# A smaller delay factor for the background scan steps of a first-layer mixer

## Chip, cores, metric

The kernel runs on one core of one Trainium2 chip. The metric is the device time of one execution in microseconds (us). Three runs of the kernel before gave 3419.37, 3421.62 and 3433.52 us, so its median is 3421.62 us.

## What is computed

Two blocks follow each other over 512 tokens of width 1024 (`x`) with 256 context tokens beside them in the first. The change touches only the first layer of the first block, whose mixer is a spatial gate beside a bidirectional linear recurrence (8 heads of 64, two directions, context first, then `x`). Cut to that:

```python
def rwkv7_scan(r, w, k, v, kk, b, s0):
    def step(s, inp):
        r_t, w_t, k_t, v_t, kk_t, b_t = inp
        sa = jnp.einsum('bhvk,bhk->bhv', s, kk_t)
        s = s * w_t[:, :, None, :] - sa[..., None] * b_t[:, :, None, :] + v_t[..., None] * k_t[:, :, None, :]
        return s, jnp.einsum('bhvk,bhk->bhv', s, r_t)
...
def mixer_ab(hc, hl, need_ctx, w_in, w_out, ...):
    pc, pl = hc @ w_in, hl @ w_in
    bc, bl = rwkv_bidir(pc, pl, ...)          # the scans, both directions, then norm, bonus and gate
    yl = jnp.concatenate([spatial_gate(pl, ...), bl], axis=-1) @ w_out
    yc = jnp.concatenate([spatial_gate(pc, ...), bc], axis=-1) @ w_out
```

## The kernel before

The recurrence is done in chunks of 64 tokens with a triangular inverse in each (`inverse`, L731 to L749). Two heads make a pair, and a pair with both its directions is a strand, `rwkv_pair`: a Python generator that emits one step (some 16 matmuls of 64x64 and their evictions) and then yields two numbers, the TensorE time of the step and the time until its results are there. There are four strands, one for each pair. Their products with the weights (`mmacc`, L344, L347 and L348: three matmuls for each K-tile) run in the foreground, in float32r pieces.

A planner inside the kernel mixes the two. It keeps a clock `now` of its own, in modelled ns; a step of the inverse, for one, yields 320 and 1000. After each K-tile of products `tick` adds the time of its matmuls, and every strand whose due time has come emits its next step there. After a step the due time is set by one line, where `s[3]` is the factor of that strand and LF is 2.5:

```python
s[2] = self.now + r[1] * LF * s[3]
```

Five parts follow each other on TensorE, and I call them by these names:

- **Projection part**: `proj(1)` to `proj(3)`, the products of the pairs 1 to 3; strands 0 and 1 begin beside them, with the factor SL1.
- **Gate part**: `gate_part`, the products of the spatial gate, beside the same strands and factor.
- **Early part**: no products. `finish(early)` runs strands 0 and 1 to their end (factor SLO, 1.2) together with strands 2 and 3 (factor 1.0) and with `ada_steps`, which reads the modulation weights in 40 steps of 1 MB (`ar`, L556 and L558). In this part the planner emits whatever is due first, one step behind the other.
- **Output part**: the product with `ab_w_out` over the first six of its eight K-tiles (`gemm_out`), beside what is left of strands 2 and 3 and of `ada_steps`.
- **Rest**: `drain` runs strands 2 and 3 to their end, and the last two K-tiles of the output product follow.

The order on TensorE is the planner's: the first matmul of each step and each K-tile is pinned in place, and the scheduler of the framework fills in the others. TensorE takes its queue in that order, so a step whose inputs are late holds up all that stands behind it. SP is the queue that issues nearly all DMAs, also in order: weights (`wr`), modulation weights (`ar`) and the strands' blocks (`kq`, `cut`). Slabs of the output weights and the modulation weights share two buffers `wr`; every third modulation step takes a pair `wh`, `wl` of the buffers for split weights instead.

Of the kernel before, what the change touches and what calls it, by code (L numbers as in the profile page):

```python
# [649 lines left out]

NB = 2
SLO = 1.2
SL1 = 0.9


class Chunk:
# [125 lines left out]
def mixer_ab(K, X, CH, x):  # L782
# [91 lines left out]
    def strand(pair, **pages):  # L874
        K.lend([envs[pair]], **pages)
        K.background(envs[pair], rwkv_pair(K, CH, pair, rkv, lo, Y), 8000, SL1 if pair < 2 else 1.0,
                     heirs[pair] if pair < 2 else None)
# [27 lines left out]
    for e in envs[:2]:  # L905
        K.give_back(e)

    K.env = Env((5, 6, 7), [], [], [])
    ks = range(KD - 2)
    y = gemm_out(K, K.ins["ab_w_out"][0], reload_split(K, Y, SEGS, ks), SEGS, ks)  # L910
# [11 lines left out]
def rwkv_pair(K, CH, p, rkv, lo, Y):  # L922

    nc = K.nc
    upt = K.p1(name="up")
    up = {}
    for i, key in enumerate(("b_w_up", "b_a_up")):
        up[key] = upt[:, i * P:(i + 1) * P]
        nc.gpsimd.dma_start(up[key], K.ins[key][0, :, :, p * P:(p + 1) * P].rearrange("d r c -> (d r) c"))
    y = {s: K.pg(s, name="y") for s, _ in SEGS}  # L930
    bon = {s: K.pg(s, name="bon") for s, _ in SEGS}
    pads = CH.pads(K.p1)

    SV, NV = [[K.p1(name=x) for _ in range(2)] for x in ("SV", "NV")]
    for h, t in enumerate(SV):
        nc.gpsimd.memset(t[64 * h:64 * h + 64], 0.0)
    seen = set()
    blk = C64 * NB
    ends = []

    def end(s, sel):
        ends.append(False)
        return rwkv_end(K, p, s, sel, y[s], bon[s], rkv, ends, len(ends) - 1)

    for s, n in reversed(SEGS):
        for i in range(0, n, blk):
            loc = ((s, i), (s, n - blk - i))
            out = {}
            yield from rwkv_prep(K, CH, p, loc, rkv, lo, up, bon, seen, out, pads, SV, NV)
            yield from rwkv_scan(K, loc, y, seen, out, SV, NV)  # L950
            if s == "c" and i == n - blk:
                K.background(K.env, end(s, slice(0, 2)))
            elif s == "l" and i == n - 2 * blk:
                K.background(K.env, end(s, slice(1, 3)))
    K.free(upt, *pads, *SV, *NV)
    yield from end("l", slice(0, 4, 3))
    while not all(ends):
        yield 0, 500
    for s, n in SEGS:
        K.free(bon[s])  # L960
        if p >= 2 and s == "l":
            Y[s][4 + p] = K.common_split(y[s])
        else:
            Y[s][4 + p] = K.out_dram(y[s], n)
# [1267 lines left out]
def program(K):  # L2232
# [8 lines left out]
    X = K.normed(x, SEGS, K.gs_pre(0, SEGS, "nmp0", 1), {s: K.modv(0, s, 0) for s, _ in SEGS})  # L2241
    K.vec_setup(layer1_vecs(K))
    y, xd = mixer_ab(K, X, CH, x)
    K.vec_setup(ffn_vecs(K, 0))

# [61 lines left out]
```

## Time and profile before

| | |
|---|---|
| runs | 3419.37, 3421.62, 3433.52 us (median 3421.62) |
| profiled execution | 3418.44 us, of which the profile's span is 3416.7 us |
| TensorE busy | 3151.7 us (92%) |
| VectorE, ScalarE, GpSimd busy | 2122.4 us (62%), 1269.4 us (37%), 614.0 us (18%) |
| mean granted TensorE clock | 0.953 |
| projection, gate, early, output part, rest, last two K-tiles | 123 to 250, to 394, to 700, to 801, to 848, to 866 us |

The parts were placed by the starts of their first and last products in the trace. The busy times of TensorE come from modelled ends of pipelined matmuls, so only its longer pauses show as idle. A matmul of the strands in float32 stands as two records in the trace, so a step that the order below prints as x8 is an x16 there.

### The profile page before, as it was taken

The numbers are of one execution on the slowest core, as the hardware profiler recorded it, in microseconds if no ns is written. First come the engines' busy times: TensorE is split into PE (matmuls) and PEld (weight loads), VectorE is DVE, ScalarE is ACT, GpSimd is POOL, SyncE is SP. The second block draws the span as 40 slices with busy tenths as digits, with TensorE's granted clock in tenths as the row PEclk, the third lists the DMA queues.
The fourth block names the chain that finished last, engine by engine and source line by source line (L and its number), as shares of the span: only waits on it lengthen the run. The fifth ranks groups of instructions, "written<-read, shape, count | busy, mean of one in ns | idle before, by whom it ended". The sixth has DMA issues, their size and how long they took to land.

```text
span 3416.7 us, 61935 instructions
## 1 busy us (share of the span) xinstructions
PE 3151.7 (92%) x25042; PEld 2476.2 (72%) x25042; DVE 2122.4 (62%) x4318; ACT 1269.4 (37%) x2679; POOL 614.0 (18%) x762
## 2 busy tenths in 40 slices
PE   7999898888899999989888999988999899999988
PEld 4878676667688888868765888767667567766756
DVE  4444565645855555685666576677777666677665
ACT  4333343333432222364433332352433335233332
POOL 4111222211000000010010000005156000525500
PEclk8999998999999999999998999989999899999979
DMA  6432554431222222122222223232232343123332
GB/s 228 141 94 70 166 167 155 139 112 52 73 72 68 72 73 97 57 73 69 81 78 82 91 87 132 78 99 78 69 103 95 104 138 102 57 69 108 102 115 90
DMA packets 313570, 336.10 MB, mean 98 GB/s; under 512 B 26542, under 2 KB 259132, under 8 KB 313284
## 3 DMA queue, kind: packets, MB, share of 16 engines
q1 hardware_dynamic: 311172, 329.69, 30.0%
q8 instruction: 197, 3.23, 0.4%
q0 software_dynamic: 2112, 2.45, 0.3%
q14 instruction: 89, 0.73, 0.1%
HBM read 282.13 MB, written 49.94 MB: 97 GB/s over the span
## 4 chain that ended last, share of the span: by engine, by line
PE 61%; issue 18%; DVE 14%; ACT 3%; DMA 3%; POOL 0%; SPq 0%; DVEq 0%; POOLq 0%; ACTq 0%
PE mm L344 14%; PE mm L347 13%; PE mm L348 13%; DVE cfa L1794 3%; PE ps L739 2%; PE ps L748 2%; PE ps L1192 2%; DVE wl L81 2%; PE ps L1137 1%; PE ps L558 1%; PE ps L1719 1%; PE ps L2133 1%; DMA ld<-sp 1%; PE ps L2160 1%; PE ps L1701 1%
## 5 line engine op out<-in xcount | busy, mean ns | idle before, releaser
L344 PE MATMUL mm<-hl,wh 128*128 128x512 f32 (+1 forms) x3296 | 1249.6, 383 | 56.0 <-DVE qkv L1794 15.2
L347 PE MATMUL mm<-hl,wh 128*128 128x512 f32 (+1 forms) x3296 | 1225.8, 372 | 1.6 <-DVE hl L487 1.6
L348 PE MATMUL mm<-hl,wl 128*128 128x512 f32 (+1 forms) x3296 | 1218.5, 372 | 0.0
L344 PEld LDWEIGHTS mm<-hl,wh 128*128 128x128 f32 x3296 | 631.1, 192 | 192.8 <-issue 33.2
L348 PEld LDWEIGHTS mm<-hl,wl 128*128 128x128 f32 x3296 | 631.4, 192 | 114.6 <-issue 2.8
L347 PEld LDWEIGHTS mm<-hl,wh 128*128 128x128 f32 x3296 | 633.2, 192 | 106.3 <-DVE hl L487 3.4
L80 ACT ACTIVATE wh<-wr 128x512 fp32r<-128x512 f32 (+3 forms) x718 | 367.9, 561 | 704.2 <-PE mm L347 614.3
L81 DVE TENSOR_TENSOR wl<-wr,wh 128x512 fp32r<-128x512 f32 (+3 forms) x718 | 435.7, 640 | 230.1 <-ACT wh L80 205.2
L1372 DVE SCALAR_TENSOR_TENSOR cv<-mm,vecs,cv 128x441 f32<-128x441 f32 (+2 forms) x352 | 242.9, 692 | 94.3 <-ACT cv L1360 88.2
L1423 POOL MEMSET gwh<- 128x1024 f32 x3 | 2.9, 955 | 969.2 <-PE mm L347 969.2
L1794 DVE SCALAR_TENSOR_TENSOR cfa<-ld,vecs,cfa 128x497 f32<-128x497 f32 (+14 forms) x160 | 162.1, 1013 | 13.2 <-ACT cfa L1788 11.0
L1962 POOL TENSOR_SCALAR tap<-ld,vecs 128x498 f32<-128x498 f32 (+4 forms) x80 | 150.6, 1882 | 63.9 <-PE ps L2046 29.8
L1395 DVE TENSOR_TENSOR fy<-fy,mm 128x512 f32<-128x512 f32 x96 | 55.2, 577 | 126.3 <-PE mm L348 125.5
L1963 POOL TENSOR_TENSOR cfa<-cfa,tap 128x498 f32<-128x498 f32 (+4 forms) x80 | 112.1, 1401 | 5.3
L743 ACT ACTIVATE pad<-ps 128x256 f32<-128x256 f32 (+1 forms) x100 | 46.7, 468 | 155.5 <-PE ps L739 155.0
L2138 ACT ACTIVATE u<-ps,beT 64x128 f32<-64x128 f32 x128 | 46.2, 362 | 131.3 <-DVE u L2137 130.6
L1374 ACT ACTIVATE cv<-cv,vecs 128x256 f32<-128x256 f32 (+1 forms) x66 | 43.0, 652 | 132.1 <-DVE cv L1372 77.2
L749 DVE TENSOR_TENSOR cut<-cut,ps 128x256 f32<-128x256 f32 x120 | 49.3, 413 | 54.0 <-PE ps L748 53.2
L2137 DVE TENSOR_SCALAR u<-ps,kdT 64x128 f32<-64x128 f32 x128 | 44.5, 349 | 58.4 <-PE ps L2133 44.4
L1378 DVE TENSOR_TENSOR cv<-cv,mm 128x512 f32<-128x512 f32 x66 | 39.5, 599 | 65.5 <-ACT cv L1374 36.2
L425 PE MATMUL ps<-sq,one 128*128 128x512 f32 (+1 forms) x132 | 62.6, 609 | 15.8 <-ACT sq L395 13.7
L731 POOL TENSOR_TENSOR pad<-L,zm 128x512 f32<-128x512 f32 x40 | 54.4, 1360 | 113.4 <-PE ps L739 84.0
(479 smaller groups left out, 4418.9 us busy)
## 6 DMA issues: line engine op xcount, KB each, us to landing
ar<-in_ada_w_dram SPq DMA_DIRECT2D x96, 512.0 KB, 5.2
wr<-in_ffn_up_dram SPq DMA_DIRECT2D x44, 1024.0 KB, 5.0
wr<-in_w_in_dram SPq DMA_DIRECT2D x28, 1024.0 KB, 5.2
ld<-sp SPq DMA_DIRECT2D x84, 256.0 KB, 4.5
wr<-in_w_in_dram SPq DMA_DIRECT2D x32, 512.0 KB, 3.6
xsp<-x SPq DMA_DIRECT2D x48, 256.0 KB, 2.0
x<-xsp SPq DMA_DIRECT2D x48, 256.0 KB, 3.5
wr<-in_ffn_down_dram SPq DMA_DIRECT2D x20, 512.0 KB, 3.7
```

Source lines behind the costliest of these rows:

```text
L80: nc.scalar.activation(h[:, q:e], src, AF.Copy)
L81: nc.vector.tensor_tensor(l[:, q:e], src, h[:, q:e].bitcast(F32), SUB)
L344: mm = nc.tensor.matmul(ps[:m, :n], wh[:, i, :m], H[:, :n], start=first and i == 0, stop=False)
L347: nc.tensor.matmul(ps[:m, :n], wh[:, i, :m], L[:, :n], start=False, stop=False)
L348: nc.tensor.matmul(ps[:m, :n], wl[:, i, :m], H[:, :n], start=False, stop=last and i == nk - 1)
L739: nc.tensor.matmul(ps[r, u * 64:u * 64 + 64], L[r, u], W[r, u], start=True, stop=True)
L748: nc.tensor.matmul(ps[r, u * 64:u * 64 + 64], X[r, u], Z[r, u], start=True, stop=True)
L1192: nc.tensor.matmul(ps[hs[h], d], lhsT(d, h), rhs(d, h), start=first and i == 0 and d == 0, stop=last and i == len(parts) - 1, skip_group_c ...
L1372: nc.vector.scalar_tensor_tensor(t3[:, ro, co], a3[:, ri, ci], tap(ky, kx, ff), t3[:, ro, co], MUL, ADD)
L1794: nc.vector.scalar_tensor_tensor(dst[:, a:b], src[:, a + o:b + o], taps[j], dst[:, a:b], MUL, ADD)
L1962: nc.gpsimd.tensor_scalar(x[:, a:b], src[:, a + o:b + o], taps[j], None, MUL)
L1963: nc.gpsimd.tensor_tensor(g[:, a:b], g[:, a:b], x[:, a:b], ADD)
```

## The change

The factor SL1 of strands 0 and 1 in the projection and gate parts falls from 0.9 to 0.7, and before the output part the factor of all that is still in the background (strands 2 and 3 and the modulation steps) is set from 1.0 to 0.6. Nothing else is edited; no operation is added or removed.

```diff
@@ -650,7 +650,8 @@
 NB = 2
 SLO = 1.2
-SL1 = 0.9
+SL1 = 0.7
+SLE = 0.6
...
@@ -905,6 +906,8 @@
     for e in envs[:2]:
         K.give_back(e)
 
+    for x in K.back:
+        x[3] = SLE
     K.env = Env((5, 6, 7), [], [], [])
     ks = range(KD - 2)
     y = gemm_out(K, K.ins["ab_w_out"][0], reload_split(K, Y, SEGS, ks), SEGS, ks)
```

In the changed kernel the lines from L653 on stand one lower, and those from L909 on three. Counting the matmuls other than products in the two orders, part by part (the modulation steps' own in brackets), and the runs of them that stand between products:

| part | matmuls before | after | runs before | after |
|---|---|---|---|---|
| projection | 484 | 596 | 45 | 54 |
| gate | 612 | 792 | 52 | 66 |
| early | 2928 (144) | 2252 (112) | 1 | 1 |
| output | 365 (16) | 783 (48) | 37 | 52 |
| rest | 370 | 336 | 9 | 7 |
| sum | 4759 | 4759 | 144 | 180 |

TensorE in the output part, beside the second half of the second slab of output weights, before (`mm` is the product's tile, `ps` that of a strand, L739 and L748 the two matmul groups of the inverse):

```order
L348 MATMUL mm_1440_9576<-hl_1381_9179,wl_1439_9571 128x512
L739 MATMUL ps_1443_9601<-cut_728_4235,cut_725_4232 64x64 x8
L344 MATMUL mm_1440_9576<-hl_1386_9190,wh_1438_9570 128x512
L347 MATMUL mm_1440_9576<-hl_1387_9191,wh_1438_9570 128x512
L348 MATMUL mm_1440_9576<-hl_1386_9190,wl_1439_9571 128x512
L748 MATMUL ps_1444_9616<-cut_716_4223,bk_1322_8865 64x64 x8
L344 MATMUL mm_1440_9576<-hl_1391_9201,wh_1438_9570 128x512
```

and after, beside the same half slab, where L558 is a modulation step and L1140, L1162, L740 and L749 are the strands' (L1137, L1159, L739 and L748 before):

```order
L1162 MATMUL ps_1428_9465<-bk_1406_9285,kq_1402_9249 64x64 x8
L749 MATMUL ps_1429_9475<-cut_769_4675,bk_1377_9095 64x64 x8
L344 MATMUL mm_1418_9365<-hl_1325_8714,wh_1415_9358 128x256
L347 MATMUL mm_1418_9365<-hl_1325_8714,wh_1415_9358 128x256
L348 MATMUL mm_1418_9365<-hl_1325_8714,wl_1416_9359 128x256
L1140 MATMUL ps_1430_9488<-cut_781_4687,bk_1406_9285 64x64 x8
L1140 MATMUL ps_1431_9489<-cut_781_4687,bk_1406_9285 64x64 x8
L558 MATMUL ps_1359_8928<-ar_1432_9508,csil_68_341 32x512 x4
L740 MATMUL ps_1433_9515<-cut_773_4679,cut_770_4676 64x64 x8
L740 MATMUL ps_1434_9528<-cut_781_4687,cut_778_4684 64x64 x8
L344 MATMUL mm_1418_9365<-hl_1330_8725,wh_1415_9358 128x256
```

Where one step stood alone between two K-tiles, two to five now stand in one run.

SP in the output part, before, from the modulation weights to the third slab of output weights (`wr`); L1049, L1050 and L1053 load the strands' blocks, L974 and L975 are loads of a strand's end, L646 reloads `x`:

```order
L556 DMA ar_1404_9292<-in_ada_w_dram 128x1024
L556 DMA ar_1420_9413<-in_ada_w_dram 128x1024 x2
L319 DMA wr_1425_9459<-in_ab_w_out_dram 128x6x256
L1050 DMA cut_731_4238<-rkv_189_811 128x128
L620 DMA sp_1363_9140<-y_348_1639 128x512
L1050 DMA cut_731_4238<-rkv_189_811 128x128
L974 DMA cut_730_4237<-rkv_205_827 128x256
L646 DMA x_1654_10962<-xsp_182_796 128x256
L626 DMA ld_1390_9199<-sp_1363_9140 128x512
L646 DMA x_1653_10960<-xsp_182_796 128x256
L556 DMA ar_1433_9524<-in_ada_w_dram 128x1024 x2
L319 DMA wr_1452_9677<-in_ab_w_out_dram 128x6x256
```

and after, up to the same third slab (L1053, L1056 and L977 are L1050, L1053 and L974 before):

```order
L1056 DMA cut_778_4684<-rkv_197_819 64x128
L1056 DMA cut_779_4685<-rkv_197_819 64x128
L1056 DMA cut_778_4684<-rkv_197_819 64x128
L1056 DMA cut_779_4685<-rkv_197_819 64x128
L1053 DMA cut_776_4682<-rkv_187_809 128x128
L977 DMA cut_775_4681<-rkv_203_825 128x256
L556 DMA ar_1432_9508<-in_ada_w_dram 128x1024 x2
L1056 DMA cut_779_4685<-rkv_197_819 64x128
L1056 DMA cut_780_4686<-rkv_197_819 64x128
L1056 DMA cut_779_4685<-rkv_197_819 64x128
L1056 DMA cut_780_4686<-rkv_197_819 64x128
L319 DMA wr_1437_9547<-in_ab_w_out_dram 128x6x256
```

Ahead of these rows stand one more load and the modulation step that takes `wh` and `wl` buffers (`ar_1421`, `ar_1422`). The third slab now stands behind eleven loads of blocks and two modulation steps, where before it stood behind one modulation step and loads of `x` and `y`.

## Rows read from the trace of the kernel before

**Rows 1.** Busy time of each engine in the six stretches (us, TensorE first).

```profile
core 0: us, PE busy (x) PEld busy (x) DVE busy (x) ACT busy (x) POOL busy (x), PEclk, DMA share, GB/s
123.00:250.00 127.00, 127.00 (x1476) 101.96 (x1475) 62.57 (x134) 46.27 (x110) 23.94 (x36) 1.00 0.36 109
250.00:394.00 144.00, 139.87 (x1736) 115.69 (x1735) 65.44 (x157) 59.24 (x136) 30.73 (x57) 1.00 0.29 88
394.00:700.00 306.00, 264.57 (x5569) 201.32 (x5569) 192.66 (x488) 118.50 (x365) 86.94 (x157) 0.94 0.50 163
700.00:801.00 101.00, 92.45 (x1032) 72.31 (x1029) 38.67 (x98) 31.02 (x85) 12.57 (x22) 0.95 0.33 103
801.00:848.00 47.00, 38.22 (x662) 31.51 (x661) 28.10 (x73) 12.91 (x38) 11.25 (x15) 0.89 0.03 8
848.00:866.00 18.00, 16.30 (x77) 12.88 (x76) 16.32 (x38) 11.95 (x29) 0.00 (x0) 0.92 0.40 132
```

**Rows 2.** Waits of TensorE in the early part, longest in total.

```profile
engine line waited for: us in total, times, longest us
PE ps L739 <- DVE cut L749: 8.3, 5, 4.7
PE ps L1137 <- DVE kq L1118: 5.8, 6, 1.5
PE ps L1137 <- ACT cut L743: 3.7, 1, 3.7
PE ps L1040 <- DVE cut L1224: 3.0, 2, 2.5
```

**Rows 3.** All waits of TensorE in the output part.

```profile
PE mm L344 <- ACT hl L324: 6.9, 1, 6.9
PE ps L1137 <- DVE kq L1118: 1.7, 1, 1.7
```

**Rows 4.** Timeline, output part: one strand step between products, and its eviction.

```profile
start us, us, engine line op out<-in xcount [idle before <-releaser]
744.60 0.40 PE L348 MATMUL mm<-hl,wl 128*128 128x512 f32 x1
...
744.92 0.68 PE L739 MATMUL ps<-cut,cut 64*64 64x64 f32 x16
...
745.53 0.50 PE L344 MATMUL mm<-hl,wh 128*128 128x512 f32 x1
...
745.71 0.39 ACT L743 ACTIVATE cut<-ps 128x256 f32<-128x256 f32 x1 [1.10 <-PE ps L739]
745.87 0.39 PE L347 MATMUL mm<-hl,wh 128*128 128x512 f32 x1
...
746.10 0.39 PE L348 MATMUL mm<-hl,wl 128*128 128x512 f32 x1
```

**Rows 5.** Timeline of TensorE, early part: steps behind each other.

```profile
442.09 0.68 PE L739 MATMUL ps<-cut,cut 64*64 64x64 f32 x16
442.70 0.49 PE L1192 MATMUL ps<-cut,cut 128*64 128x64 f32 x7
...
444.79 0.68 PE L748 MATMUL ps<-cut,bk 64*64 64x64 f32 x16
445.40 0.45 PE L1192 MATMUL ps<-cut,rk 128*64 128x64 f32 x8
```

**Rows 6.** Modulation steps on TensorE: groups of the early part, then of the output part.

```profile
L558 PE MATMUL ps<-ar,csil 128*32 128x512 f32 x296 | 47.2, 668 | 2.2 <-DMA ar<-in_ada_w_dram 2.2
L558 PE MATMUL ps<-ar,csil 128*32 128x512 f32 x24 | 3.2, 605 | 0.0
```

**Rows 7.** DMA issues of the page (us to landing), SP and ScalarE in the output part.

```profile
ar<-in_ada_w_dram SPq DMA_DIRECT2D x96, 512.0 KB, 5.2
...
730.66 0.38 SPq L319 DMA_DIRECT2D wr<-in_ab_w_out_dram  x1
...
764.70 2.51 SPq L1053 DMA_DIRECT2D cut<-rkv  x4
...
735.29 0.94 ACT L80 ACTIVATE wh<-wr 128x384 fp32r<-128x384 f32 x2 [1.39 <-DMA wr<-in_ab_w_out_dram]
```

## Prediction

> **What bounds the kernel now.** I read the windows of the first layer's mixer first, because the change moves work between its parts and does no other work. In the projection and gate parts TensorE has next to nothing to spare: 127.0 of 127 us busy and 139.9 of 144 [rows 1]. The early part is where it pauses, 264.6 of 306 us, so 41.4 us idle; the output part has 101 − 92.5 = 8.5 us idle, the rest 47 − 38.2 = 8.8 us [rows 1]. The list of waits says what the pauses of the early part are: many short ones, behind VectorE's subtraction in the inverse, behind VectorE's scaling ahead of the block products, behind ScalarE's eviction [rows 2]. These are strand steps that come to the head of TensorE's queue before their inputs are there. In the output part there are only two waits: 6.9 us for the split of the last reloaded tile `hl`, which has to wait for strand 1's end, and 1.7 us [rows 3]. So TensorE bounds all of these parts, and the change can win only what it takes from 41.4 + 8.5 + 8.8 us of pauses, less what a new order costs.
>
> **What moves.** The table of the two orders shows it: 676 of 2928 matmuls leave the early part, 32 of them those of 8 modulation steps (four each); 112 go to the projection part, 180 to the gate part, 418 to the output part, and the rest loses 34. The sum, 4759, stays.
>
> *The matmuls themselves: 0.* A step of sixteen records takes 745.53 − 744.92 = 0.61 us until the next product can start [rows 4], and in the early part 442.70 − 442.09 = 0.61 us and 445.40 − 444.79 = 0.61 us until the next step [rows 5]. What is saved early is paid beside the products at the same price. The early part ran at a mean granted clock of 0.94, a mix of the two levels, 2.4 and 1.2 GHz, and the others at 1.00 and 0.95 [rows 1]; so the 644 strand matmuls moved may win a little: the busy time that is not modulation, 264.6 − 47.2 = 217.4 us over 2784 matmuls, is 0.078 us each, against 0.61/8 = 0.076 us. That is 644 x 0.002 = 1.3 us, and I leave it to the range.
>
> *Entries: +7 us.* Each run of strand steps between products costs something on its two sides. Products of 512 columns start 746.10 − 745.87 = 0.23 us apart; the step began 744.92 − 744.60 = 0.32 us after the product ahead, and the product behind it took 745.87 − 745.53 = 0.34 us [rows 4]. So a run costs 0.09 + 0.11 = 0.20 us. The runs rise from 144 to 180, because the steps now stand several in one run: 36 x 0.20 = +7.2 us.
>
> The Trainium skill, TensorEngine Tiling (Array Packing), Key Properties, states that changing the tiling mode, unlike changing the tile, drains TensorE; a strand's 64x64 steps between 128x128 products do that twice per run. The trace agrees with a price there, the 0.20 us of [rows 4]. By that rule read step by step, each of the steps that move pays a drain of its own: the 710 matmuls that come to the three parts with products are 678/8 + 32/4 = 93 steps, 93 x 0.20 = +18.6 us in place of +7.2, and the forecast would be 11 us higher.
>
> *Modulation steps: −1.7 us.* In the early part a step of eight records takes 47.2 us x 8/296 = 1.28 us, beside the products 3.2 x 8/24 = 1.07 us [rows 6]: 8 x 0.21.
>
> *Pauses of the early part: −9.6 us.* With 2252/2928 of its matmuls in the same kind of order, I take 41.4 x 676/2928 = 9.6 us off. The bounds are 0, if the pauses hang on a few places that stay (the first blocks of strands 2 and 3, the ends of strands 0 and 1), and half of them, 20.7 us, if it is the steps of strands 0 and 1 that stop TensorE, of which fewer are left there.
>
> *Pauses beside the products: 0.* The new factors bring a step's successor nearer, and TensorE would stop there if the input were late. What has to fit between them is the eviction: ScalarE's ends at 745.71 + 0.39 = 746.10, so 0.57 us after the last record's slot ended at 745.53 [rows 4]. After a step of the inverse (320 and 1000) the planner still leaves 1000 x 2.5 x 0.6 = 1500 of its ns in the output part, 1750 in the other two, and its clock runs slow against the chip's, since it counts a step as 320 ns that took 0.61 us. The eviction fits two to three times. I take 0; the bound is 0.3 us, half an eviction, for each of 93 steps, +28 us.
>
> *The wait for `hl`: 0.* Strand 1's end, spill, reload and split stay as they are, and the order, added up at the prices above (0.23 us a product, half of it for 256 columns, 0.076 us a strand matmul), puts some 8 us of other work between its last matmul and the product that waits, about as before; the bound is −6.9 us, if it is covered.
>
> *DMA in the output part: 0, and up to +21 us.* No byte is added, but twelve modulation steps load there where four did. The slab of output weights behind them has the same two buffers. Its load took 735.29 − 730.66 = 4.6 us from issue until ScalarE could begin to split it, and a half of a modulation step lands 5.2 us after its issue [rows 7]. After `ar_1421`, which must wait until a product tile has given back its `wh`, SP issues eleven loads of blocks at 2.51/4 = 0.63 us each [rows 7], some 7 us with the rest, and then the third slab: 7 + 4.6 + 1 us for its split, against the products and steps that the order puts between, which add up to 15.7 us in the same way. That leaves 3 us. The modulation step itself has 5.8 us of work ahead of it for a load of 5.2. I take no stall, and as a bound four of 5.2 us.
>
> *Rest: 0.* It loses 34 of 370 matmuls; its 8.8 us of pauses fall by at most a tenth.
>
> The sum is +7.2 − 1.7 − 9.6 = −4.1 us on the profiled execution's 3418.4, that is 3414.3. That execution lies 3.2 us under the median of the runs, 3421.6; the same −4.1 from there is 3417.5. I say 3416.
>
> **The rivals.**
>
> *The pauses give way (faster).* The early part loses half its pauses, because its waits [rows 2] are those of strands 0 and 1, and the wait for `hl` [rows 3] is covered by the longer run of steps ahead of it: 7.2 − 1.7 − 20.7 − 6.9 = −22 us, 3396 to 3400. For it speaks that VectorE and ScalarE, which the waits name, are busy only 193 and 119 of 306 us there [rows 1], so that the pauses are a matter of order alone; against it that strands 2 and 3 keep their factor in that part, and the same four strands with the same engines wait on each other.
>
> *Late loads (slower).* SP's queue in the output part is longer by eight modulation steps, and the slabs and modulation weights wait for each other's buffers. Each load that misses its place stops TensorE for up to 5.2 us; from five of them on, +26 − 4 = +22 us, the kernel is slower by more than 0.5%, at 3440. For it speak the margins of 3 and 0.6 us above; against it that the load with the 1.39 us wait on ScalarE [rows 7] stopped TensorE not at all [rows 3].
>
> *Steps too early (slower).* At the 0.3 us bound above, +28 − 4 = +24 us, 3442; from 0.23 us a step on it shows. Against it speaks that the waits of the output part hold only one behind a strand's input [rows 3], with 1.7 us, at a factor of 1.0.
>
> *Every moved step pays its own entry*, whether another stands beside it or not: −4 + 11 = +7 us, 3425, which is no change that can be told. The early part speaks against it: a step of one kind behind another takes no longer than 0.61 us [rows 5].
>
> **How the numbers follow.** A measurement of this kernel tells about 0.5%, 17 us, from no change. My forecast, the sum with its small terms off by a few us, has a chance of 0.57 and its own range of 3405 to 3428; every step paying its entry 0.05. Both are within 0.5%, and so is the edge of the next: pauses giving way 0.24. Late loads have 0.08, steps too early 0.06. Within 0.5%: 0.61; faster: 0.25, with a little from the forecast's lower edge; slower: 0.14. The range of 8 in 10 runs from 3397, where the faster case centres, to 3436, short of the two slower ones.
>
> **What would show it.** In the profile after, the early part should last about 306 − 676 x 0.104 = 236 us (306 us over 2928 matmuls is 0.104 each), the projection and gate parts 10 and 17 us longer, the output part about 42 us longer, and each of these three about as busy as before. The early part's idle time should be near 32 us. If the kernel is faster, that idle time is well below 25 us, or the 6.9 us wait is gone. I am wrong on the other side if the list of waits in the output part shows TensorE behind `wh`, `ar` or an eviction for more than 15 us in all.

## Result and profile after

The changed kernel takes 3447.95 us (median of 6 runs, 3444.88 to 3455.24) against 3423.63 us before (6 runs): ratio 1.0070, 95% interval 1.0052 to 1.0088. It is slower by 24 us (0.7%). The profiled execution takes 3450.46 us, 32.0 more than that of before, which lies 5 us under its own median.

The windows of the mixer, now cut exactly at the last and first product on either side of the early part. First before:

```profile
core 0: us, PE busy (x), PEclk, DMA share, GB/s
117.30:251.60 134.30, 134.30 (x1525) 1.00 0.37 111
251.60:372.40 120.80, 120.80 (x1376) 1.00 0.26 81
372.40:694.90 322.50, 276.94 (x5831) 0.94 0.50 160
694.90:862.00 167.10, 149.78 (x1847) 0.93 0.27 84
862.00:890.00 28.00, 20.17 (x54) 0.88 0.37 133
```

and after; the lines are the projection part, the gate part, the early part, output part with rest, and the way to the next layer's first products:

```profile
116.30:260.30 144.00, 144.00 (x1706) 1.00 0.36 106
260.30:407.00 146.70, 144.24 (x1765) 0.99 0.24 75
407.00:682.60 275.60, 235.22 (x4491) 0.86 0.47 148
682.60:886.40 203.80, 191.37 (x2610) 0.94 0.37 115
886.40:918.00 31.60, 22.81 (x54) 0.73 0.32 114
```

The parts beside products got longer by 9.7, 25.9 and 36.7 us, and the early part gave back 46.9: the last product of the mixer ends 24.4 us later (886.4 against 862.0). Another 4 us of the two profiled runs lie in the last line, where the same 54 records ran at 0.73 instead of 0.88. The run with the second half of the change alone, which is no slower than before, has 0.72 there, so that belongs to this one execution of before and not to the change.

The line to look at is the early part. Its idle time fell from 45.6 to 40.4 us, its matmuls by 676 of 2928, but its granted clock fell from 0.94 to 0.86. At before's price the 2252 that stay would be busy for 276.94 x 2252/2928 = 213.0 us; they were busy for 235.2. Groups of the early part after:

```profile
line engine op names shapes xcount | busy us, mean ns | idle before us <-releasers
L558 PE MATMUL ps<-ar,csil 128*32 128x512 f32 x224 | 39.6, 711 | 0.9 <-DMA ar<-in_ada_w_dram 0.9
L1140 PE MATMUL ps<-kq,bk 64*64 64x128 f32 x384 | 27.8, 322 | 5.6 <-DVE kq L1121 4.3 <-DVE rk L1147 1.4
L749 PE MATMUL ps<-pad,bk 64*64 64x64 f32 x448 | 26.8, 241 | 0.7 <-ACT pad L744 0.7
L740 PE MATMUL ps<-cut,pad 64*64 64x64 f32 x448 | 25.6, 245 | 3.4 <-DVE cut L750 3.4
```

and two of the same groups before (L1137 is L1140 after, L748 is L749):

```profile
L1137 PE MATMUL ps<-kq,bk 64*64 64x128 f32 x480 | 30.5, 291 | 11.2 <-DVE kq L1118 5.8 <-ACT cut L743 3.7 <-DVE gn L1002 0.7
L748 PE MATMUL ps<-pad,bk 64*64 64x64 f32 x576 | 30.3, 227 | 0.6 <-DVE bk L742 0.6
```

These kinds became longer: 711 ns against 668 [rows 6], 322 against 291, 241 against 227. How that comes about is seen around 594 us:

```profile
585.00:593.80 8.80, 8.39 (x188) 1.00 0.79 260
593.80:596.70 2.90, 0.05 (x1) 0.92 0.33 114
596.70:613.30 16.60, 16.60 (x140) 0.50 0.33 104
613.30:620.00 6.70, 5.81 (x162) 1.00 0.09 22
```

The timeline names the pause in the second line:

```profile
596.65 1.22 PE L996 MATMUL ps<-y,heads 128*128 128x256 f32 x2 [2.87 <-ACT cut L1045]
```

TensorE waits 2.87 us for ScalarE, and behind the pause it is busy for all of 16.6 us at half its clock, 1.2 GHz of 2.4. The Trainium skill, TensorE: Matmul & The Clock Gate, section "HAM oscillation — how this bites in real kernels", describes the like: where TensorE waits for a DMA ahead of each batch of matmuls, each batch starts at half rate. The trace agrees in kind, with 0.50 behind the pause, but here the wait is for an engine and shorter than the waits in the page's example. If the pause brings the fall, its own 2.9 us are the smaller part of its price: 16.6 us at half rate are 8.3 us of work. In the early parts of the two traces 16 of 17 falls begin within or soon after a pause of more than 1.1 us; of the 14 pauses of over 2 us all but one have such a fall, of the 13 shorter ones three.

That the longer records come from the clock, the trace shows directly. The modulation steps after, in the full-clock stretch from 585 to 593 us and in the half-clock one from 597 to 613:

```profile
L558 PE MATMUL ps<-ar,csil 128*32 128x512 f32 x8 | 1.1, 604 | 0.0
L558 PE MATMUL ps<-ar,csil 128*32 128x512 f32 x16 | 3.9, 1059 | 0.0
```

and before, from 500 to 515 us (clock 1.00) and from 519.9 to 526.5 us (0.50):

```profile
L558 PE MATMUL ps<-ar,csil 128*32 128x512 f32 x16 | 2.1, 605 | 0.0
L558 PE MATMUL ps<-ar,csil 128*32 128x512 f32 x8 | 1.9, 1060 | 0.0
```

At a given level the records are as long in one kernel as in the other; more of them fall into half clock. Added up, TensorE is at half clock for 37.5 us of the early part before, in seven stretches of at most 6.8 us, and for 79.6 us after, in ten stretches of up to 17.1 us. The 42.1 us more are an estimated 21 us of work, which fits the 235.2 - 213.0 = 22.2 above. It is not the profiled execution alone: the clock over the whole kernel is 0.945 to 0.948 in all six runs of the changed kernel, and 0.948 to 0.955 in the 65 runs of the kernel before that were measured beside the experiments. From the means, 0.947 and 0.951, the changed kernel is some 30 us longer at half clock, by which I put the clock's share at about 15 of the 24 us.

All waits of TensorE in the output part after:

```profile
engine line waited for: us in total, times, longest us
PE mm L344 <- ACT wh L80: 3.3, 1, 3.3
PE ps L749 <- ACT cut L744: 2.1, 1, 2.1
PE ps L984 <- ACT bon L999: 1.8, 1, 1.8
PE ps L1140 <- DVE kq L1121: 1.0, 1, 1.0
PE ps L740 <- DVE cut L750: 0.2, 1, 0.2
```

8.4 us in all, where it was 8.6 [rows 3]: the wait for `hl` is gone, and others of the same sum are there.

### The profile page after: what moved, and what is told of

Its sections match the earlier page's. It is cut to its first block, busy times and chain, and to the rows that moved or that the text cites. A ratio compares the mean times of both kernels' runs of the same rounds, so it can differ in the third digit from the quotient of the medians.

```text
span 3448.8 us, 61962 instructions
## 1 busy us (share of the span) xinstructions
PE 3192.0 (93%) x25042; PEld 2498.7 (72%) x25042; DVE 2121.4 (62%) x4318; ACT 1276.3 (37%) x2684; POOL 618.0 (18%) x762
```

## Experiments

The theory tested was that the lower clock of the early part is what made the change slower. Its rivals were the output part (crowding by SLE) and the order itself (longer steps and entries, whatever the clock shows). Each run's windows give the early part and what follows up to the mixer's last product. The kernel before was measured again beside every set of runs, with medians of 3426.3 to 3428.9 us, so versions are compared by their ratios to it.

**The two halves of the change.** First SL1 alone:

```diff
 SL1 = 0.7
-SLE = 0.6
+SLE = 1.0
```

> The first factor alone (SL1 0.7), the output part at its old 1.0. The order has the projection, gate and early parts exactly as in the changed kernel (596, 792 and 2252 strand matmuls), and 525 + 77 + 517 in the output part and behind it, where the changed kernel has 783 + 16 + 320. Theory (the early part of the thinned order runs at a lower granted clock, and this is the loss): early part about 275 us at a clock near 0.86, kernel 3440 to 3455 us. Rival (the output part's crowding by SLE is the loss): gate and projection parts cost 36 us more, the early part gives back 47, and the kernel comes to 3415 to 3425 us.

3457.01 us, ratio 1.0089 (1.0073 to 1.0105), 2 us over the range of the theory:

```profile
408.20:673.60 265.40, 225.47 (x4492) 0.90 0.49 154
673.60:892.20 218.60, 196.08 (x2610) 0.91 0.34 107
```

The loss comes with SL1. This run is also a comparison that needs no edit: its early part holds the same matmuls in the same order as the changed kernel's (counted kind by kind, no record stands more than four places from where it stands there), with the same idle time (39.9 and 40.4 us). At 0.90 in place of 0.86 its busy time is 225.5 in place of 235.2 us, and the part is 10.2 us shorter. Behind it, SLE saves 218.6 - 203.8 = 14.8 us once SL1 has brought the work there; an estimated 7 of them are the clock of that stretch, 0.91 against 0.94. SLE alone:

```diff
-SL1 = 0.7
+SL1 = 0.9
 SLE = 0.6
```

> The second factor alone (SLE 0.6), SL1 at its old 0.9. Projection, gate and early parts as in the kernel before; in the output part 633 strand matmuls stand beside the products instead of 365, and 102 behind instead of 370. Theory (the loss is the early part's clock under SL1): early part about 322 us at 0.94, the output part some 30 us longer, the rest some 30 us shorter or a little more, since its pauses go: kernel 3410 to 3425 us. Rival (crowding of the output part): the output part's waits behind reloads, modulation weights or evictions rise by over 15 us, kernel above 3435 us.

3429.30 us, ratio 1.0002 (0.9992 to 1.0013): no change, though 4 us over the range I gave.

```profile
372.60:694.20 321.60, 278.61 (x5832) 0.94 0.51 161
694.20:857.90 163.70, 149.24 (x1847) 0.95 0.28 87
...
858.00:889.00 31.00, 22.44 (x54) 0.72 0.32 114
```

The early part is that of before, and with 268 matmuls moved from behind to beside the products the stretch behind it is 3.4 us shorter (the last line is the way to the next layer's products, spoken of above). Its clock, 0.95 in place of 0.93, is an estimated 3.5 us, so the move itself shows no gain and no loss: the output part is not crowded.

**Holding the clock up.** A matmul of the identity, whose result is overwritten by the step behind it, ahead of every step of the inverse in the early part; in the changed kernel and in the one before:

```diff
             ps = K.ps()[:, :n]
+            if K.fill: nc.tensor.matmul(ps[:, :P], K.ident, K.ident, start=True, stop=True)
             for u in range(nu):
...
+    K.fill = True
     K.finish(early)
+    K.fill = False
```

> The changed kernel with one 128x128 matmul of the identity ahead of each step of the inverse in the early part (123 more matmuls; their result is overwritten), to keep TensorE's activity up there. Each costs an estimated 0.2 to 0.4 us, 25 to 50 us in all. Theory: the early part's clock rises from 0.86 towards 0.95 or more, the strand records return to about 47 ns, and the part grows by clearly less than the filler's own time: about 0 to 25 us, kernel 3448 to 3473 us. Rival (the longer records have nothing to do with the clock, but with the order of the steps): clock as before or not, the records stay near 52 ns and the kernel grows by all of the filler's time, 3475 to 3500 us.

> The same filler in the kernel before (152 more matmuls in its early part), as the measure of what a filler costs where the clock is already 0.94. Theory: 152 x 0.2 to 0.4 us less a small gain from the last 0.06 of clock: 3440 to 3470 us, so that the distance between the two kernels with fillers, 24 us without, shrinks to within 10 us or turns round. Rival: the distance stays 24 us, less some 8 us for the 29 fillers fewer.

In the changed kernel 3442.61 us, 5 us under the theory's range, ratio 1.0046 (1.0028 to 1.0064):

```profile
408.00:680.60 272.60, 261.46 (x4809) 0.99 0.48 151
680.60:874.50 193.90, 183.41 (x2540) 0.98 0.38 119
```

In the kernel before 3470.55 us, ratio 1.0130 (1.0107 to 1.0152):

```profile
373.40:737.40 364.00, 345.32 (x6136) 0.97 0.45 142
737.40:904.80 167.40, 153.02 (x1845) 0.91 0.27 83
```

The same filler lengthens before's early part by 41.5 us and shortens the changed one's by 3.0, although it adds work to both. The distance of 24 us between the kernels turned into 28 the other way; 34 fillers more in before, at 0.40 us, are 14 of these 52. Against the changed kernel's 1.0070 (1.0052 to 1.0088) the full filler's 1.0046 is not clearly less.

The fillers do more than fill: the framework's scheduler places the matmuls that are not pinned anew around them. With the full filler 54% of the early part's records stand more than 16 places, a step's length, from where the changed kernel has them; with the half filler below it is 36%, with the float32r one 20%. So a filler's effect on the clock is not separated from that of the order it makes.

With every second filler only:

> The changed kernel with the filler ahead of every second step of the inverse alone (61 in place of 123, 0.40 us each as measured in the run with all of them, 47.5 us over 118). Theory: the clock of the early part comes to lie between 0.86 to 0.90 and 0.99, the filler's 24 us go half into the pauses, half are paid by faster records: part 265 to 276 us, kernel 3437 to 3448 us. Rival (the filler only filled pauses, the clock comes by chance): clock 0.86 to 0.90, kernel 3448 to 3462 us.

3437.78 us, ratio 1.0027 (1.0014 to 1.0041), by the ratios 0.4% faster than without filler:

```profile
407.40:668.20 260.80, 234.75 (x4607) 0.97 0.50 156
```

Groups of its early part (modulation step, block products, and the filler):

```profile
L559 PE MATMUL ps<-ar,csil 128*32 128x512 f32 x224 | 35.1, 636 | 0.3 <-DMA ar<-in_ada_w_dram 0.3
L1144 PE MATMUL ps<-kq,bk 64*64 64x128 f32 x384 | 25.1, 289 | 1.7 <-DVE kq L1125 1.7
L748 PE MATMUL ps<-ident 128*128 128x128 f32 x116 | 28.0, 327 | 1.6 <-ACT cut L745 1.6
```

The modulation and block records are back at before's lengths or below (636 and 289 ns), the part is 14.8 us shorter than without the 58 fillers, each two records, that it holds. The counterpart is a filler in float32r, at every step:

```diff
+        self.fx = self.const([P, P], F32R, name="fx")
+        nc.scalar.activation(self.fx, self.ident, AF.Copy)
...
+            if K.fill: nc.tensor.matmul(ps[:, :P], K.fx, K.fx, start=True, stop=True)
```

> The changed kernel with the filler at every step of the inverse in the early part, but the identity in float32r, which takes one pass over its columns instead of the two records that a float32 one leaves: 0.1 to 0.2 us each, 12 to 24 us. Theory: if that is activity enough to hold the clock at 0.95 or more, the filler hides in the pauses and the records return to 47 ns: part 250 to 262 us, kernel 3422 to 3436 us; if the clock stays at 0.86 to 0.90, 3446 to 3460 us. Rival (the clock has no part in it): kernel 3450 to 3465 us whatever the clock shows.

3462.52 us, ratio 1.0097 (1.0072 to 1.0123), not clearly above the changed kernel's 1.0070:

```profile
409.30:701.30 292.00, 264.33 (x4607) 0.88 0.45 140
```

and the group of the block products in it:

```profile
L1147 PE MATMUL ps<-kq,bk 64*64 64x128 f32 x384 | 29.0, 315 | 4.5 <-DVE kq L1128 4.5
```

The clock stays at 0.88, the records stay long (315 ns), and the part grows by 16.4 us. The kernel's time lies 2.5 us over the theory's range for a clock that stays and inside the rival's, so by itself it decides nothing. Both fillers fill pauses (idle time 26.0 and 27.7 us in place of 40.4); time was won only with the one that went with a higher clock. Why the two differ in that is open. That the clock makes the longer records rests not on this pair but on the records at either level, shown with the result, and on the same order at 0.86 and 0.90.

**Is it a few long pauses?** The same float32 filler only ahead of pauses that the trace shows, as many as fit into each (`PLUG` lists tiles and counts):

```diff
     def ps(self):
-        return self.bank(self.env.ps, "ps")
+        t = self.bank(self.env.ps, "ps")
+        for _ in range(PLUG.get(self.uid, 0)):
+            self.nc.tensor.matmul(t[:, :P], self.ident, self.ident, start=True, stop=True)
+        return t
```

> The changed kernel with the identity matmul of the runs before (0.40 us each, float32, result overwritten) only ahead of 15 of the 18 pauses of more than 0.75 us that the changed kernel's trace shows in its early part, as many as fit into each pause, 67 in all (27 us). The claim to test: the granted clock falls behind single long pauses (the trace shows it at 0.50 behind pauses of 1.3 to 3.2 us), not because the part is thinner on the whole. If so, filling the long pauses alone brings the part's clock from 0.86 to 0.95 or more, costs little, and the part takes 245 to 262 us in place of 276; kernel 3420 to 3437 us. Rival (the clock follows the work as a whole, or the pauses move elsewhere): clock under 0.92, part 270 us or more, kernel 3440 to 3470 us.

> The same in the kernel before: 72 identity matmuls (29 us) ahead of 15 of its 17 pauses of more than 0.75 us in the early part. Claim: the clock rises from 0.94 to 0.97 or more, half of (0.97 - 0.94) x 2 x 322 = 19 us at the low level is won, less what does not fit into the pauses: part 312 to 325 us, kernel 3412 to 3428 us. Rival: the filler is paid in full, part 340 us or more, kernel 3440 us or more.

In the changed kernel 3442.39 us, ratio 1.0055 (1.0043 to 1.0067):

```profile
408.80:663.80 255.00, 224.93 (x4628) 0.98 0.50 160
663.80:865.10 201.30, 188.33 (x2608) 0.97 0.37 116
```

The part did what was claimed: clock 0.98, 20.6 us shorter. The kernel missed its range and lies in the rival's: by the ratios it is not clearly faster than the changed kernel. Its profiled execution (3436.28 us) is 14.2 us faster, but 8.6 of these are the spread between runs: it lies 6.1 under its median, and the changed kernel's 2.5 over its own. And of the 21.3 us by which its mixer ends sooner 7 are lost behind the mixer, where its trace has 281.4 us at half clock in place of 263.8, an estimated 8.8 us of work. In the kernel before 3434.30 us, ratio 1.0030 (1.0018 to 1.0042), a miss:

```profile
370.30:703.20 332.90, 297.85 (x5994) 0.95 0.49 155
```

There the clock stays at 0.95 and the part is 10.4 us longer. With 29 us of filler its idle time fell only from 45.6 to 35.1 us: other pauses take the place of those filled, and with little clock to win back the filler is paid.

**Other orders.** If the clock fell because the early part is thinner, it should rise when more is left in it, and fall half as far at half the step:

```diff
-SL1 = 0.7
-SLE = 0.6
+SL1 = 1.1
+SLE = 1.0
```

> The opposite of the change: SL1 1.1 and SLE 1.0, so that 380 strand and modulation matmuls more than in the kernel before stand in the early part (3308), and 48, 114 and 202 fewer in the projection part, the gate part and behind the early part. Theory (the early part, whose clock falls as it is thinned, gives back only the 0.069 us for a matmul that the two traces show, 46.9 / 676, while the gate part charges 25.9 / 196 = 0.132 and the projection part 9.7 / 112 = 0.087): 380 x 0.069 = +26 early, -15 and -4 in the two others, -19 at 0.096 (36.9 / 384) behind: -12, and the early part's clock at 0.95 or more: 3408 to 3420 us. Rival (the clock in the early part has nothing to do with how full it is): 380 x 0.104 = +40, the sum about 0 to +3 us, 3420 to 3432 us.

3453.61 us, ratio 1.0073 (1.0055 to 1.0092). Both expectations missed:

```profile
247.40:359.40 112.00, 112.00 (x1182) 1.00 0.26 83
359.40:755.30 395.90, 334.01 (x6587) 0.87 0.46 146
```

With 380 matmuls more the clock is 0.87, the idle time 61.9 us and the part 73.4 us longer. So "thinner, hence slower" is wrong: the clock fell with a change of SL1 in either direction. Half the step (SL1 0.8, SLE 0.6):

> Half the step of the first factor (SL1 0.8) with the second as in the change (SLE 0.6): 2628 matmuls in the early part, 528 in the projection part, 664 in the gate part. Theory (a clock that falls as the part is thinned): early part's clock between 0.86 and 0.94, kernel between the two, 3430 to 3440 us. Rival (something in the order of 0.7 alone, one stall or a clock dip at one place): kernel as before, 3420 to 3428 us.

3445.26 us, ratio 1.0050 (1.0031 to 1.0068), the early part's clock between the two, the kernel 5 us over what I expected for it:

```profile
387.10:688.60 301.50, 254.85 (x5240) 0.91 0.50 156
```

Here the clock is not the whole loss. Over the six runs it is 0.949 to 0.952 for the whole kernel, as before; but the early part begins 14.7 us later (387.1 against 372.4) for 96 matmuls moved ahead of it, which at the forecast's 0.076 us would be 7.3, entries aside.

The last two change the third factor, SLO, which times the front strands inside the early part:

```diff
-SLO = 1.2
-SL1 = 0.7
+SLO = 1.0
+SL1 = 0.9
 SLE = 0.6
```

> SL1 0.9 as before, SLE 0.6, and the factor of the front strands in the early part (SLO) 1.0 in place of 1.2: another order of the same early part with 230 matmuls fewer in it (2698), the projection and gate parts as before, 669 + 296 behind where the kernel before has 365 + 370. A look for an order with fewer long pauses, and a test of what goes with the time of the early part: if the clock does, and the clock with the pauses of over 1.6 us, the part takes 0.104 us x 2698 = 281 us plus half of what the time at the low level grows over the 37.5 us of before. 8 such pauses or fewer: part under 290 us, kernel 3415 to 3428 us; 10 or more: part 295 to 305 us, kernel 3432 to 3450 us. Rival (what is placed beside the output products costs too much): kernel above 3432 us with the early part under 290 us.

> The changed kernel with SLO 1.5: projection and gate parts as in the changed kernel, its front strands held back further in the early part, which has 2549 matmuls in place of 2252, and 696 + 126 in place of 799 + 320 behind. If the lower clock belongs to this stretch of long pauses and not to the share of work placed ahead of it, it comes out with the pauses: 8 or fewer of over 1.6 us give a clock of 0.93 or more and a part under 275 us, kernel 3425 to 3437 us; 10 or more give 0.86 to 0.91, a part of 280 to 300 us and 3440 to 3460 us.

SLO 1.0 with SL1 0.9 and SLE 0.6 takes 3420.97 us, ratio 0.9982 (0.9973 to 0.9991), by 0.2% the only version faster than both kernels:

```profile
372.80:668.70 295.90, 258.14 (x5375) 0.91 0.50 155
668.70:855.40 186.70, 175.26 (x2302) 0.96 0.34 107
```

The early part, 6 us over the range for so few pauses, gives back 26.6 us for 230 matmuls, and 19.6 are paid behind it. Its idle time fell to 37.8 us. But at five pauses of over 1.6 us (eight before, nine in the changed kernel, counted from the ends and starts of TensorE's records) its clock is 0.91, under before's: the number of long pauses alone does not give the clock. SLO 1.5 in the changed kernel takes 3446.62 us, ratio 1.0060 (1.0043 to 1.0077), about as expected for its ten such pauses (the part half a us over):

```profile
408.70:709.20 300.50, 260.20 (x5082) 0.90 0.51 161
```

## Why the prediction was wrong

I said 3416, no change that can be told, and up to 3436; it is 3447.95, slower by 0.7%. Point by point:

- **The matmuls themselves, 0: this step failed.** "What is saved early is paid beside the products at the same price" holds for a step at a given clock. I then took the early part's 0.94 as a property of the part, let the moved matmuls "win a little", and left the clock to the range with 1.3 us. The clock there depends on the order that the change makes. At 0.86 the 2252 matmuls that stayed cost 235.2 - 213.0 = 22.2 us more. That is the largest part of the 28 us between the -4 forecast and the +24 measured: about 22 by the profiled executions, about 15 by the clocks of all runs. The records at either clock and the same order at 0.90 show it.
- **Pauses of the early part, -9.6:** -5.2 measured, inside the bounds. They did not give way as the faster rival had it.
- **The early part as a whole:** I expected about 236 us. Part of that was a wrong boundary: I had it begin at 394 us, but the last product of the gate part starts at 372.4, so it had 322.5 us and not 306. With 322.5/2928 = 0.110 us a matmul it would have been 248 us; it is 275.6. The same boundary made the clock term too small: the busy time from 394 us on belongs to 2636 strand matmuls (half of 5569 - 296 records) and not to 2784, which is 0.082 us each and puts the 644 moved ones at 4 us instead of 1.3.
- **Projection +10, gate +17, output +42:** +9.7, +25.9, and +36.7 for the output part together with the rest, which lost 34 matmuls. The gate part is under-sized by 9 us, the second step that failed. Its 180 matmuls (196 in one of the expectations, where a step between two parts is counted elsewhere) came at 0.144 us each, entries included; 2.5 us of it are new idle time, which I had at 0 there. What the rest is, no run separates; the run with SL1 0.8 shows the like.
- **Entries, +7.2:** not separated by any run. With half a filler the kernel is at 1.0027, 9 us over before, and some 9 us of that filler are paid (58 x 0.40 = 23, of which 14 went into pauses). But its early part is at 0.97, and at before's 0.94 it would be an estimated 8 us longer. So the rest of the sum is about +7 and not -4, near the gate part's 9; this is argued from the parts, not measured alone.
- **Steps too early and late loads:** refuted. The waits of the output part are 8.4 us, those behind `wh` 3.3 us in one. The wait for `hl` went, at the bound of -6.9, and others came in its place.
- **Every moved step pays its own entry:** that would lift all three parts with products over the forecast; only the gate part lies over it.

What stays open is why one order of the same steps draws 0.94, in both runs that have it, and others 0.86 to 0.91. Nearly all falls stand behind pauses, but the number of pauses alone doesn't order the runs.

## What to carry to other kernels

In a stretch of small matmuls with pauses a new order can bring another clock, as every other SL1 or SLO did here, and one order can differ from run to run (0.86 and 0.90): price the work that stays, not only the work that moves. Before moving work out of such a stretch, read its granted clock and price the case that it falls; in the windows after, divide busy time by the count before looking for new waits, and compare records of one kind at full and at half clock. A filler of idle time won here only where the clock was low and rose with it, and not clearly in every such case.

## What was unexpected on the chip

Behind a pause of 2.9 us TensorE stayed at 0.50 for 16.6 us though busy throughout. Two executions of the same order of matmuls had 0.86 and 0.90 in it. And with 58 float32 identity matmuls in it the part's clock was 0.97 in place of 0.86, where twice as many in float32r left it at 0.88.
